# Output projection of a hybrid attention layer as seven block products in place of eight

## The chip, the cores and the metric

The kernel runs on one core of a Trainium2 chip. The metric is the device time of one execution in microseconds (us), lower is better. TensorE is written PE, VectorE DVE, ScalarE ACT, GpSimd POOL and SyncE SP, as in the profile.

## What is computed

One decoder layer on 512 tokens of width 1024, in fp32 (cut to what matters):

```python
def hybrid_layer(x, p_i, norm_g, w_in, sinks, rel_bias, w_out, ple_g, w_ple_gate, w_ple_proj):
    h = rms_norm(x, norm_g)
    proj = h @ w_in
    a_q, a_k, a_v, a_g, b_q, b_k, b_v, b_g = jnp.split(proj, offs, axis=-1)
    a_out = swa_attention(a_q, a_k, a_v, sinks, rel_bias[:, :8])      # window 128, 8 query heads
    b_out = moba_attention(b_q, b_k, b_v, rel_bias[:, 8:])            # blocks of 256, 8 heads
    mixed = jnp.concatenate([a_out * jax.nn.silu(a_g), b_out * jax.nn.silu(b_g)], axis=-1)
    x = x + mixed @ w_out                                             # (512 x 1024) @ (1024 x 1024)
    gate = jax.nn.sigmoid(rms_norm(x, ple_g) @ w_ple_gate)
    return x + (p_i @ w_ple_proj) * gate
# reference(): one such layer, then rms_norm(x, final_norm)
```

The change concerns `mixed @ w_out`, the output projection.

## The kernel before, in words

**Products of fp32.** Every fp32 operand is cut into two fp32r tiles: `hi`, a rounded copy, and `lo`, what is left. A product is then three matmuls (`three`, L136): hi by hi, hi by lo, lo by hi, added in one PSUM bank. One matmul takes a 128x128 stationary piece (128 tokens of 128 rows of K) and 512 columns.

**Weights** (class `Weights`, L85). `load` has SP fetch a raw block of 1 MB (128 x 2048 elements) into one of the two buffers of pool `wraw`. `split` cuts a quarter of it: ACT copies it into `hi` (L116) and DVE subtracts to get `lo` (L118). With `engines="AP"` every second `lo` cut goes to POOL instead; the default is `"AD"`.

**Stages.** (1) RMSNorm of x, its transposes, first columns of the input projection. (2) The rest of the input projection, 88 pieces of which stand in the list `stream`, woven into the attention: `run` takes the next pieces off the list, and `Pace` says how many after each step of attention, first 20 steps of the sliding-window attention (`swa_step`), then 38 of the block-sparse one (`moba_step`). A sliding-window step is a chain over all engines: scores on PE (L562), softmax with its normalisation on POOL (the "norm add" below, L574: the sum with the sink's term) and DVE (L575, L577), transposes on PE (L585), the product with V on PE (L602). Results go to the tiles `O`, and `silu_gate` (L539) multiplies them with the gate, six of the eight times on POOL. (3) The output projection: the gated `O` are split into `acts`; then eight K chunks of `w_out` times four token tiles times two halves of 512 columns times three matmuls, 192 in all. First the left half of the columns with four banks open and the K loop outside (`accs`), then the right half token tile by token tile. Each token tile then is added to x (`x2_evac`, L861), squared and normalised (`h2_norm`, L867), and transposed on PE (`h2_trans`, L874) while the next tile's matmuls run. Between the matmuls `ahead3` (L837) splits the next weights. (4) The gate projection on the same pattern, sigmoid, the last norm, the store.

**What sets the order.** PE's and SP's instructions stand in the order of the program (`MANUAL`, L34); DVE's, ACT's and POOL's are ordered by a scheduler when the kernel is built. Each engine works through its own queue in order, so a waiting instruction holds up all that stands behind it. A DMA waits at the engine that issues it: SP for all loads, POOL for the ten moves of `kt` (L514).

Of the kernel before, what the change touches and what calls it, by code (L numbers as in the profile page):

```python
# [10 lines left out]
F32 = mybir.dt.float32  # L11
# [5 lines left out]
P = 128  # L17
# [21 lines left out]
def hybrid_layer_kernel(  # L39
# [45 lines left out]
    class Weights:  # L85


        def __init__(self, name, srcs, a=KC, pool=None, cuts=4, engines="AD"):
            self.name, self.srcs, self.a, self.cuts, self.engines = name, srcs, a, cuts, engines
            self.pool = pool or whl  # L90
            self.done, self.raw, self.flat = 0, None, None

        def load(self):
            if self.raw is not None:
                return
            self.raw = wraw.tile([P, 2048], F32, name="raw_" + self.name, tag="raw")
# [39 lines left out]
    def three(acc, sh, sl, mh, ml, first, last):  # L136
        nc.tensor.matmul(acc, sh, mh, start=first, stop=False)  # L137
        nc.tensor.matmul(acc, sh, ml, start=False, stop=False)  # L138
        nc.tensor.matmul(acc, sl, mh, start=False, stop=last)  # L139
# [13 lines left out]
    d_tab = dram.tile([HA + HB, JT], F32, name="d_tab")  # L153

# [232 lines left out]
    opool = ctx.enter_context(ExitStack())  # L387
    with ExitStack() as ph2:
# [13 lines left out]
        O = [op.tile([P, SEQ], F32, name=f"O_{c}") for c in range(8)]  # L402
# [299 lines left out]
        make_va(akv[1])  # L702

# [103 lines left out]
        for c in range(KC):  # L807
            if c >= 6:
                silu_gate(c)
            split_T(acts[:, c, 0, :], acts[:, c, 1, :], O[c])  # L810


    with ExitStack() as ph3:
        def pool3(name, bufs):
            return ph3.enter_context(tc.tile_pool(name=name, bufs=bufs, reuse_waits="tile"))

        whl2 = pool3("whl2", 2)
        xq = pool3("xq", 1)
        ep = pool3("ep", 2)

        g_ple = xq.tile([P, D], F32, name="g_ple")
        nc.sync.dma_start(g_ple, bcast(ple_norm, D))
        g_fin = xq.tile([P, D], F32, name="g_fin")
        nc.sync.dma_start(g_fin, bcast(final_norm, D))
        x2 = []
        for t in range(NT):
            x_t = xq.tile([P, D], F32, name=f"x2_{t}")
            nc.sync.dma_start(x_t, x2d[t])
            x2.append(x_t)
        h2 = xq.tile([P, KC, 2, SEQ], F32R, name="h2")  # L830
# [175 lines left out]
```

## Time and profile before

| | |
|---|---|
| device time, median of 3 runs | 315.89 us (315.51 to 315.95) |
| the profiled execution | 315.71 us, of which the span of the profile is 314.0 us |
| PE busy, mean granted clock | 304.7 us (97% of the span), 0.996 |
| DVE, ACT, POOL busy | 219.3, 187.6 and 57.9 us |
| DMA | 37.61 MB, 120 GB/s over the span |
| output projection | first matmul at 215.85 us, first matmul of the gate projection at 262.05 us |

The span runs from the first to the last instruction that the profile shows. PE is busy almost all of it, and its busy time is pipelined: a matmul that is shown with 0.39 us starts 0.23 us after the one before it, so counts are to be multiplied with the distance of starts, not with durations.

### The profile page before, as it was taken

To read this page: it belongs to the slowest core of one execution; us is meant where nothing else is said; L and a number is where in the kernel's file an instruction comes from. 1 tells how busy PE (TensorE), PEld (TensorE's weight loads), DVE (VectorE), ACT (ScalarE), POOL (GpSimd) and SP (SyncE) were. 2 spreads that over 40 slices of the span, in tenths; PEclk is the share of its full clock that TensorE was granted. 3 is DMA by queue.
4 is the path that set the end of the run, shared out by engine and by line. 5 is a ranking of instruction groups with operands and counts; after the bars stand their busy time and mean duration, and the time that the engine had idled before them with its cause. 6 is when DMAs were issued, how large, how long until landed. Compare 5 with 4: busy or idle time off the path is not lost.

```text
span 314.0 us, 4729 instructions
## 1 busy us (share of the span) xinstructions
PE 304.7 (97%) x1651; PEld 260.5 (83%) x1651; DVE 219.3 (70%) x514; ACT 187.6 (60%) x420; POOL 57.9 (18%) x112
## 2 busy tenths in 40 slices
PE   8999999999999999999999999999999999999991
PEld 6788788888899878899888888888888888888890
DVE  2885867888877877478879797759167756582544
ACT  3756657656574865578668697798058323651441
POOL 1430102434544284100000100030000110000010
PEclk9999999999999999999999999999999999999998
DMA  6953487140405061951442603003965610000113
GB/s 217 400 188 106 144 223 228 46 136 1 134 3 200 3 177 23 265 163 45 134 100 50 187 0 137 0 0 91 397 234 221 208 58 0 2 0 0 69 68 134
DMA packets 33208, 37.61 MB, mean 120 GB/s; under 512 B 1416, under 2 KB 24976, under 8 KB 33184
## 3 DMA queue, kind: packets, MB, share of 16 engines
q1 hardware_dynamic: 32240, 34.47, 33.6%
q0 software_dynamic: 800, 2.62, 3.6%
q8 instruction: 13, 0.21, 0.3%
q10 hardware_dynamic: 144, 0.21, 0.2%
q14 instruction: 11, 0.09, 0.1%
HBM read 32.52 MB, written 2.16 MB: 110 GB/s over the span
## 4 chain that ended last, share of the span: by engine, by line
PE 82%; DVE 5%; ACT 4%; issue 4%; POOL 2%; DMA 1%; SPq 0%; ACTq 0%; POOLq 0%
PE acc L457 10%; PE acc L458 10%; PE acc L459 10%; PE acc L137 8%; PE acc L138 8%; PE acc L139 8%; PE acc_ple L284 4%; PE acc_akv L303 4%; PE oaccb L652 3%; PE Sb L622 3%; PE tpb L642 3%; PE S L562 2%; PE accv L137 2%; PE accv L139 2%; PE accv L138 2%
## 5 line engine op out<-in xcount | busy, mean ns | idle before, releaser
L137 PE MATMUL acc<-hi_wg,h 128*128 128x512 f32 (+1 forms) x72 | 26.5, 368 | 0.0
L138 PE MATMUL acc<-lo_wg,h 128*128 128x512 f32 (+1 forms) x72 | 26.3, 366 | 0.0
L139 PE MATMUL acc<-hi_wg,h 128*128 128x512 f32 (+1 forms) x72 | 26.3, 366 | 0.0
L457 PE MATMUL acc<-acts,hi_bkq 128*128 128x512 f32 x64 | 25.5, 399 | 0.0
L457 PE MATMUL acc<-acts,hi_aqg 128*128 128x512 f32 x64 | 25.4, 396 | 0.0
L458 PE MATMUL acc<-acts,hi_bkq 128*128 128x512 f32 x64 | 25.1, 393 | 0.0
L459 PE MATMUL acc<-acts,lo_bkq 128*128 128x512 f32 x64 | 25.1, 393 | 0.0
L137 PE MATMUL acc<-hi_wo,acts 128*128 128x512 f32 x64 | 25.1, 393 | 0.0
L458 PE MATMUL acc<-acts,hi_aqg 128*128 128x512 f32 x64 | 25.0, 391 | 0.0
L459 PE MATMUL acc<-acts,lo_aqg 128*128 128x512 f32 x64 | 24.9, 390 | 0.0
L139 PE MATMUL acc<-hi_wo,acts 128*128 128x512 f32 x64 | 24.9, 390 | 0.0
L138 PE MATMUL acc<-lo_wo,acts 128*128 128x512 f32 x64 | 24.9, 389 | 0.0
L625 ACT ACTIVATE stb<-stb,nmb 128x128 f32<-128x128 f32 (+3 forms) x32 | 17.9, 558 | 4.6 <-DVE nmb L623 4.2
L593 POOL TENSOR_SCALAR_AFFINE_SELECT pta<-pta 128x512 fp32r<-128x512 f32 x24 | 16.9, 705 | 17.6 <-DVE pta L144 15.8
L144 DVE TENSOR_TENSOR pt<-tpb,pt 128x384 fp32r<-128x384 f32 (+1 forms) x24 | 14.4, 600 | 7.6 <-ACT pt L143 7.4
L143 ACT ACTIVATE pt<-tpb 128x384 fp32r<-128x384 f32 (+1 forms) x24 | 12.6, 524 | 10.7 <-PE tpb L642 10.5
L137 PE MATMUL accv<-hi_bv,acts 128*128 128x256 f32 x64 | 18.4, 287 | 0.4 <-DVE q L505 0.4
L568 ACT ACTIVATE st<-st,nm 128x257 f32<-128x257 f32 (+1 forms) x32 | 15.2, 477 | 5.8 <-DVE nm L565 5.8
L139 PE MATMUL accv<-hi_bv,acts 128*128 128x256 f32 x64 | 18.1, 283 | 0.0
L138 PE MATMUL accv<-lo_bv,acts 128*128 128x256 f32 x64 | 18.1, 282 | 0.0
L850 ACT ACTIVATE sq<-x 128x512 f32<-128x512 f32 x15 | 9.5, 631 | 14.1 <-DVE x L912 11.2
L514 POOL DMA_DIRECT2D kt<-kt x10 | 5.5, 553 | 64.4 <-DVE kt L144 61.3
(166 smaller groups left out, 858.1 us busy)
## 6 DMA issues: line engine op xcount, KB each, us to landing
raw_aqg<-in_w_in_dram SPq DMA_DIRECT2D x8, 512.0 KB, 4.9
raw_bkq<-in_w_in_dram SPq DMA_DIRECT2D x8, 512.0 KB, 4.6
raw_wo<-in_w_out_dram SPq DMA_DIRECT2D x4, 1024.0 KB, 8.2
raw_wg<-in_w_ple_gate_dram SPq DMA_DIRECT2D x4, 1024.0 KB, 5.0
kt<-kt POOLq DMA_DIRECT2D x10, 256.0 KB, 3.2
x_t<-in_x_dram SPq DMA_DIRECT2D x4, 512.0 KB, 7.8
raw_bv<-in_w_in_dram SPq DMA_DIRECT2D x2, 1024.0 KB, 5.2
b_b<-d_tab SPq DMA_DIRECT2D x8, 256.0 KB, 5.6
```

Of the source, the lines that this page charges most:

```text
L137: nc.tensor.matmul(acc, sh, mh, start=first, stop=False)
L138: nc.tensor.matmul(acc, sh, ml, start=False, stop=False)
L139: nc.tensor.matmul(acc, sl, mh, start=False, stop=last)
L143: nc.scalar.activation(hi, src, AF.Copy)
L144: nc.vector.tensor_sub(lo, src, hi.bitcast(F32))
L284: nc.tensor.matmul(pacc[t, n], (pTl if j == 1 else pTh)[:, k, tok(t)], (wpl if j == 2 else wph)[:, n, k], start=k == 0 and j == 0, stop=k ...
L457: nc.tensor.matmul(acc, w.hi[:, k, cs], acts[:, k, 0, :], start=k == 0, stop=False)
L458: nc.tensor.matmul(acc, w.hi[:, k, cs], acts[:, k, 1, :], start=False, stop=False)
L459: nc.tensor.matmul(acc, w.lo[:, k, cs], acts[:, k, 0, :], start=False, stop=k == KC - 1)
L568: last_exp[0] = nc.scalar.activation(st[:, s, lo_k:257], st[:, s, lo_k:257], AF.Exp, bias=nm[:, s:s + 1], scale=-1.0, accum_out=sm[:, s:s ...
L593: nc.gpsimd.affine_select(out=pt[:, :, b, :].rearrange("p j (s q) -> p j s q", s=2), in_=pt[:, :, 1, :].rearrange("p j (s q) -> p j s q", ...
L625: last_exp[0] = nc.scalar.activation(st[:, :w], st[:, :w], AF.Exp, bias=nm, scale=-1.0, accum_out=sm)
```

## The change

The output projection is taken as a product of 2 x 2 blocks: tokens in two halves of 256, K and columns in two halves of 512 each. In place of eight block products it makes seven, of sums and differences of blocks (Strassen's scheme in the form that shares sums). With X the gated activations and W the blocks of `w_out`:

- Four weight sums are made in DRAM, in `d_sum` 1 to 4 (512x512 fp32, 1 MB each). SP copies a block there, DRAM to DRAM; POOL then adds another block by an accumulating DMA. `d_sum2` starts as a copy of `d_sum1`, `d_sum4` as one of `d_sum2`. These six steps (`sum_steps`) are put between the pieces of `stream`, at the places 16, 30, 60, 76, 160 and 172.
- Four differences of activation blocks are made on POOL (`sub`, L961): eight subtractions of 128x2x256 elements. `operand` then cuts each block that a product takes into hi and lo (ACT and DVE), some of it during the products. `O` becomes one tile `mixed`.
- Seven products `w1, w2, w5, w6, w3, w7, w4`, each two token tiles by four K chunks by three matmuls: 168 in place of 192, still of 512 columns. The accumulators of `w1` go on under `w6`, `w7` and `w4`, those of `w5` under `w3`; a partial result is added into x where each product ends, so 14 additions to x in place of 8.
- The raw loads are seven blocks of 1 MB in place of four, in one pool more (`wraw2`). For `w5, w6, w3, w7, w4` and the gate's weights every second `lo` cut goes to POOL (`engines="AP"`).

The core of the diff:

```diff
+    def sum_steps():
+        add = ALU.add
+        return [
+            lambda: (nc.sync.dma_start(d_sum[1], wo_block(0, 1)), nc.sync.dma_start(d_sum[3], wo_block(1, 1))),
+            lambda: (nc.gpsimd.dma_start(d_sum[1], wo_block(0, 0), accum_op=add),
+                     nc.gpsimd.dma_start(d_sum[3], wo_block(0, 1), accum_op=add)),
+            lambda: nc.sync.dma_start(d_sum[2], d_sum[1]),
+            lambda: nc.gpsimd.dma_start(d_sum[2], wo_block(1, 1), accum_op=add),
+            lambda: nc.sync.dma_start(d_sum[4], d_sum[2]),
+            lambda: nc.gpsimd.dma_start(d_sum[4], wo_block(1, 0), accum_op=add),
+        ]
...
+        steps = dict(zip((16, 30, 60, 76, 160, 172), sum_steps()))
...
+    def operand(dst, src, neg=False):
+        for h in range(2):
+            ks = slice(2 * h, 2 * h + 2)
+            hi, lo = dst[:, 0, ks, :], dst[:, 1, ks, :]
+            nc.scalar.activation(hi, src[:, ks], AF.Copy, scale=-1.0 if neg else 1.0)
+            if neg:
+                nc.vector.scalar_tensor_tensor(lo, src[:, ks], -1.0, hi.bitcast(F32), op0=ALU.mult, op1=ALU.subtract)
+            else:
+                nc.vector.tensor_sub(lo, src[:, ks], hi.bitcast(F32))
...
-        for c in range(KC):
-            if c >= 6:
-                silu_gate(c)
-            split_T(acts[:, c, 0, :], acts[:, c, 1, :], O[c])
+        operand(parts(slot[0]), X[0][0], True)
+        for c in (6, 7):
+            silu_gate(c)
+        operand(parts(slot[1]), X[0][1])
...
+        w5, w6 = summed(1, whl2, wraw2), summed(2, whl2, wraw2)
+        w3 = wide(wo, 1, "wo", engines="AP")[1]
+        w7, w4 = summed(3, whl, wraw), summed(4, whl2, wraw2)
...
+        def sub(dst, a, b):
+            for h in range(2):
+                ks = slice(2 * h, 2 * h + 2)
+                nc.gpsimd.tensor_sub(dst[:, ks], a[:, ks], b[:, ks])
+
+        def product(w, n, accs, fresh, evac, work):
+            a = parts(slot[n])
+            for i in range(2):
+                ts = tok(i)
+                for k in range(4):
+                    three(accs[i], a[:, 0, k, ts], a[:, 1, k, ts], w.hi[:, k], w.lo[:, k], fresh and k == 0, k == 3, go_on=not fresh)
+                    for f in work.get(4 * i + k, ()):
+                        f()
+                evac(i, accs[i])
...
-        accs = [bank([P, 512], "acc3", "S" if t < 2 else "acc") for t in range(NT)]
-        for k in range(KC):
-            for t in range(NT):
-                row_piece(accs[t], acts, w_late[0], t, k)
-            ahead3(1)
...
+        ab, gh = pair("S"), pair("acc")
+        product(w1, 0, ab, True, lambda i, acc: x2_add(i, 0, acc, neg=True),
+                {0: [lambda: sub(x11, x21, x11), a1], 1: [lambda: sub(x21, x21, x22)], 2: [a1], 4: [a1], 6: [a1]})
+        product(w2, 1, gh, True, lambda i, acc: x2_add(i, 0, acc, done=True),
+                {0: [lambda: operand(parts(slot[2]), x21)], 1: [a1], 2: [lambda: operand(parts(slot[0]), x22, True)],
+                 3: [lambda: sub(x22, x22, x11), a1], 5: [a1], 7: [a1]})
+        ef = pair("o")
+        product(w5, 2, ef, True, lambda i, acc: x2_add(2 + i, 1, acc),
+                {0: [lambda: operand(parts(slot[3]), x22)], 1: [lambda: sub(x12, x12, x22), a1], 3: [a1], 5: [a1],
+                 7: [a1]})
+        product(w6, 3, ab, False, lambda i, acc: x2_add(i, 1, acc),
+                {0: [lambda: operand(parts(slot[4]), x12)], 1: [a1], 3: [a1], 4: [lambda: operand(parts(slot[1]), x11)],
+                 5: [a1], 7: [a1]})
...
+        product(w3, 4, ef, False, evac3, {0: [a1], 2: [a1], 4: [a1], 6: [a1]})
+        product(w7, 1, ab, False, lambda i, acc: x2_add(2 + i, 1, acc, done=True),
+                {1: [a1], 3: [a1], 4: [tr], 5: [a1], 7: [a1]})
...
+        product(w4, 0, ab, False, evac4, {0: [tr], 1: [a1], 3: [a1], 5: [a1], 7: [a1]})
```

Three places of the queues, as the builds of the two kernels order them. The first is POOL's queue in the sliding-window attention. `st` is a step's softmax tile, `nsink` the sink's term, `pta` the transposed weights of the attention; L574 before is L613 after, L559 is L598. Before:

```order
L574 TENSOR_TENSOR st_611<-st_611 128x2x128
L559 COPY st_849<-nsink_81 128x2
L574 TENSOR_TENSOR st_650<-st_650 128x2x128
L559 COPY st_895<-nsink_81 128x2
L593 AFFINE_SELECT pta_711<-pta_711 128x2x256
```

After:

```order
L613 TENSOR_TENSOR st_613<-st_613 128x2x128
L185 DMA d_sum1_85<-in_w_out_dram 512x512
L186 DMA d_sum3_87<-in_w_out_dram 512x512
L598 COPY st_853<-nsink_81 128x2
L613 TENSOR_TENSOR st_652<-st_652 128x2x128
L598 COPY st_899<-nsink_81 128x2
L632 AFFINE_SELECT pta_713<-pta_713 128x2x256
```

Two accumulating DMAs have come between the norm adds of two successive steps; each waits at POOL until SP's copy into the same `d_sum` has landed. The third, into `d_sum2`, stands further on, right ahead of the norm add of `st_853`.

The second is SP's queue at the same time: the loads of raw weights and of bias tables (`b_a`). Before:

```order
L100 DMA raw_aqg3_598<-in_w_in_dram 128x8x128 x2
L100 DMA raw_bv0_737<-in_w_in_dram 128x8x256
L417 DMA b_a_739<-d_tab_84 128x2x256
L100 DMA raw_bkq0_934<-in_w_in_dram 128x8x128 x2
L100 DMA raw_bkq1_1096<-in_w_in_dram 128x8x128 x2
```

After:

```order
L100 DMA raw_aqg3_598<-in_w_in_dram 128x8x128 x2
L184 DMA d_sum1_85<-in_w_out_dram 512x512
L184 DMA d_sum3_87<-in_w_out_dram 512x512
L100 DMA raw_bv0_741<-in_w_in_dram 128x8x256
L456 DMA b_a_743<-d_tab_84 128x2x256
L100 DMA raw_bkq0_938<-in_w_in_dram 128x8x128 x2
L187 DMA d_sum2_86<-d_sum1_85 16x16384
L100 DMA raw_bkq1_1101<-in_w_in_dram 128x8x128 x2
```

The two first copies stand right behind the load of `raw_aqg3`; the copy of `d_sum1` to `d_sum2`, which waits for the accumulation into `d_sum1`, stands between the loads of `raw_bkq0` and `raw_bkq1`.

The third is POOL's queue from the last gates of the attention on. `rs` are sums of squares of the norm. Before:

```order
L540 TENSOR_TENSOR O_4_483<-O_4_483,G_4_2362 128x512
L540 TENSOR_TENSOR O_5_484<-O_5_484,G_5_2473 128x512
L128 TENSOR_TENSOR rs_2819<-epst_80,ssq2_2817 128x1
L128 TENSOR_TENSOR rs_2825<-epst_80,ssq2_2823 128x1
```

After:

```order
L579 TENSOR_TENSOR mixed_461<-mixed_461,G_4_2369 128x512
L579 TENSOR_TENSOR mixed_461<-mixed_461,G_5_2481 128x512
L964 TENSOR_TENSOR mixed_461<-mixed_461 128x2x256 x4
L118 TENSOR_TENSOR lo_wos1_2709<-raw_wos1_2678,hi_wos1_2708 128x512 x2
L118 TENSOR_TENSOR lo_wos2_2756<-raw_wos2_2681,hi_wos2_2755 128x512 x2
L964 TENSOR_TENSOR mixed_461<-mixed_461 128x2x256 x4
L128 TENSOR_TENSOR rs_2777<-epst_80,ssq2_2775 128x1
L128 TENSOR_TENSOR rs_2801<-epst_80,ssq2_2799 128x1
L118 TENSOR_TENSOR lo_wos4_2901<-raw_wos4_2739,hi_wos4_2900 128x512 x2
L118 TENSOR_TENSOR lo_wo11_2820<-raw_wo11_2817,hi_wo11_2819 128x512 x2
L118 TENSOR_TENSOR lo_wos3_2862<-raw_wos3_2693,hi_wos3_2861 128x512 x2
L118 TENSOR_TENSOR lo_wg00_2962<-raw_wg00_2795,hi_wg00_2961 128x512 x2
```

Where POOL had only tiny sums to do, 18 elementwise operations on 128x512 elements with two operands in SBUF now stand in its queue (the names `wos1, wos2, wos4, wo11, wos3` are those of `w5, w6, w4, w3, w7`), and two more for `wg01` behind them.

## Rows read from the trace of the kernel before

**Rows 1.** The page: busy time of each engine, and PE's granted clock.
```profile
PE 304.7 (97%) x1651; PEld 260.5 (83%) x1651; DVE 219.3 (70%) x514; ACT 187.6 (60%) x420; POOL 57.9 (18%) x112
...
PEclk9999999999999999999999999999999999999998
```
**Rows 2.** The page: the chain that ended last, by engine.
```profile
PE 82%; DVE 5%; ACT 4%; issue 4%; POOL 2%; DMA 1%; SPq 0%; ACTq 0%; POOLq 0%
```
**Rows 3.** Busy time by stretch: us, PE, PEld, DVE, ACT, POOL, clock, DMA, GB/s.
```profile
220.00:225.00 5.00, 5.00 (x23) 4.13 (x22) 1.07 (x2) 0.00 (x0) 0.00 (x0) 1.00 1.02 401
310.00:314.00 4.00, 0.00 (x0) 0.00 (x0) 0.14 (x1) 0.23 (x1) 0.00 (x0) 0.71 0.34 131
```
**Rows 4.** Timeline of PE, output projection: start, us, instruction.
```profile
215.85 0.45 PE L137 MATMUL acc<-hi_wo,acts 128*128 128x512 f32 x1
...
224.10 0.39 PE L137 MATMUL acc<-hi_wo,acts 128*128 128x512 f32 x1
...
229.54 0.39 PE L137 MATMUL acc<-hi_wo,acts 128*128 128x512 f32 x1
...
262.05 0.48 PE L137 MATMUL acc<-hi_wg,h 128*128 128x512 f32 x1
```
**Rows 5.** The chain in order of time: start, us, what (three of its transposes).
```profile
59.24 0.24 PE tp L585 x2
...
76.64 0.24 PE tp L585 x2
...
248.75 0.87 PE tp L879 x8
```
**Rows 6.** Two-operand work of 128x512: POOL's by line (ns min/median/max), DVE's by timeline.
```profile
L540 POOL TENSOR_TENSOR O<-O,G x6: 1275/1294/1792, 111.2 to 208.5; 128x512 f32<-128x512 f32 x6
...
230.25 5.06 DVE L118 TENSOR_TENSOR lo_wo<-raw_wo,hi_wo 128x512 fp32r<-128x512 f32 x8 [9.19 <-ACT hi_wo L116]
```
**Rows 7.** Timelines of DVE and POOL where both work at once, 111 to 126 us.
```profile
111.17 1.41 DVE L577 TENSOR_SCALAR st<-st,ri 128x128 f32<-128x128 f32 x1 [1.16 <-POOL st L574]
111.19 1.30 POOL L540 TENSOR_TENSOR O<-O,G 128x512 f32<-128x512 f32 x1
115.08 0.69 DVE L144 TENSOR_TENSOR kt<-acc,kt 64x512 fp32r<-64x512 f32 x1 [0.33 <-ACT kt L143]
115.31 0.65 POOL L593 TENSOR_SCALAR_AFFINE_SELECT pta<-pta 128x512 fp32r<-128x512 f32 x1
123.91 0.69 DVE L118 TENSOR_TENSOR lo_bv<-raw_bv,hi_bv 128x512 fp32r<-128x512 f32 x1
123.97 1.79 POOL L540 TENSOR_TENSOR O<-O,G 128x512 f32<-128x512 f32 x1 [4.28 <-DVE O L612]
```
**Rows 8.** Timeline of SP's DMA queue in the sliding-window attention.
```profile
44.85 1.17 SPq L100 DMA_DIRECT2D raw_aqg<-in_w_in_dram  x2
...
64.32 16.28 SPq L100 DMA_DIRECT2D raw_bkq<-in_w_in_dram  x4
```
**Rows 9.** DMA issues: what, queue, count, KB each, median us to landing.
```profile
raw_aqg<-in_w_in_dram SPq DMA_DIRECT2D x8, 512.0 KB, 4.9
...
raw_wo<-in_w_out_dram SPq DMA_DIRECT2D x4, 1024.0 KB, 8.2
```
**Rows 10.** Timelines of POOL and DVE in the sliding-window attention.
```profile
50.37 0.93 POOL L574 TENSOR_TENSOR st<-st 128x256 f32<-128x256 f32 x1 [12.48 <-ACT st L568]
54.03 0.74 POOL L574 TENSOR_TENSOR st<-st 128x256 f32<-128x256 f32 x1 [1.74 <-ACT st L568]
54.81 0.48 DVE L577 TENSOR_SCALAR st<-st,ri 128x128 f32<-128x128 f32 x2 [0.43 <-POOL st L574]
...
70.60 0.73 POOL L574 TENSOR_TENSOR st<-st 128x256 f32<-128x256 f32 x1 [2.59 <-ACT st L568]
71.37 0.48 DVE L577 TENSOR_SCALAR st<-st,ri 128x128 f32<-128x128 f32 x2
```
**Rows 11.** The page's groups: POOL's own DMA issues.
```profile
L514 POOL DMA_DIRECT2D kt<-kt x10 | 5.5, 553 | 64.4 <-DVE kt L144 61.3
```

More of the change, by code (lines that the diff above doesn't have):

```diff
@@ L134, in rstd, with three @@
         return s
[L136 to L139, printed above, removed]
+    def three(acc, sh, sl, mh, ml, first, last, go_on=False):
+        nc.tensor.matmul(acc, sh, mh, start=first, stop=False, skip_group_check=go_on)
+        nc.tensor.matmul(acc, sh, ml, start=False, stop=False, skip_group_check=go_on)
+        nc.tensor.matmul(acc, sl, mh, start=False, stop=last, skip_group_check=go_on)
     def split_T(hi, lo, src):
@@ L702, in hybrid_layer_kernel @@
         make_va(akv[1])
+        items, n = deque(stream), 0
+        stream.clear()
+        steps = dict(zip((16, 30, 60, 76, 160, 172), sum_steps()))
+        for it in items:
+            if it[0]:
+                if n in steps:
+                    add(0, steps[n])
+                n += 1
+            stream.append(it)
         class Pace:
@@ L841, in ahead3 @@
                     w.split()
-                    nx = flat_late.index(w) + 1
-                    if w.done == w.cuts and nx + 1 < len(flat_late):
-                        flat_late[nx + 1].load()
+                    if w.done == w.cuts and id(w) in follows:
+                        follows[id(w)].load()
+        load_x(0)
+        w5.load()
+        load_x(1)
+        w6.load()
+        while split_seq[0] in (w1, w2):
+            ahead3(1)
+        load_x(2)
+        load_x(3)
+        nc.sync.dma_start(g_ple, bcast(ple_norm, D))
+        nc.sync.dma_start(g_fin, bcast(final_norm, D))
+        ssq = {}
         def square(t, key, cols):
-            sq = ep.tile([P, 512], F32, name="sq2", tag="sq", bufs=1)
+            sq = ep.tile([P, 512], F32, name="sq2", tag="sg")
             ss = small.tile([P, 1], F32, name="ssq2", bufs=12)
@@ L854, in half, with row_piece, x2_add @@
             return slice(n * 512, (n + 1) * 512)
[L856 removed]
+        def row_piece(acc, t, w, k, cols=slice(0, 512)):
             ww = w[k // 4]
[L858 removed]
+            three(acc, h2[t][:, k, 0, :], h2[t][:, k, 1, :], ww.hi[:, k % 4, cols], ww.lo[:, k % 4, cols],
                   k == 0, k == KC - 1)
[L861 to L863 removed]
+        def x2_add(t, n, acc, neg=False, done=False):
+            xs = x2[t][:, half(n)]
+            if neg:
+                nc.vector.tensor_sub(xs, xs, acc)
+            else:
+                nc.vector.tensor_add(xs, acc, xs)
+            if done:
+                square(t, 0, half(n))
+        h2 = [slot[(2, 3, 4, 1)[t]].rearrange("p (k j n) -> p k j n", k=KC, j=2) for t in range(NT)]
         h2t = {}
@@ new lines, in product, with pair @@
+        def product(w, n, accs, fresh, evac, work):
[7 more added lines that the diff above has]
+                evac(i, accs[i])
+        def pair(tag):
+            return [bank([P, 512], "acc3", tag) for _ in range(2)]
```

98 lines of the change are left out of this document (53 added, 45 removed).

## Prediction

> **What bounds the kernel now.** The page comes first: PE is busy for 97% of the span, at full granted clock in every slice but the last [rows 1], and the chain that ended last runs 82% through PE [rows 2]. So a matmul that is left out ends the kernel earlier by one distance of starts, as long as the other engines have PE's operands ready. That distance is read from PE's timeline in the stage that changes [rows 4]: from 224.10 to 229.54 us lie 24 matmuls, 5.44 us, 0.2267 each. The whole stage, 215.85 to 262.05, is 46.2 us; 192 x 0.2267 is 43.5, and three blocks of transposes of 0.87 [rows 5] make 46.1. PE waits for nothing there; whatever becomes late there is paid in full.
>
> The second view is what the other engines do beside it. POOL is busy for 18% of the span [rows 1], so it looks free. What a POOL operation costs and what it does to DVE stands in rows 6 and 7. POOL's six multiplications of 128x512 with two operands in SBUF took 1.275 us at the least, DVE's subtractions of that size 5.06 / 8 = 0.63 [rows 6]. Where they meet they take turns [rows 7]: a DVE operation of 128x128, of which two take 0.48 elsewhere [rows 10], started 0.02 ahead of such a POOL operation and took 1.41, until that had ended; a POOL operation that started 0.06 behind a DVE subtraction took 1.79. A DVE subtraction with one operand in PSUM beside POOL kept its 0.69. So POOL's time on such work is not beside DVE's two-operand time, it is added to it.
>
> The third view is the sliding-window attention, where new DMAs are put. POOL's norm add of a step ends at 54.77, DVE's scaling at 55.29 [rows 10], and PE takes the transposes at 59.24 [rows 5]: 3.95 us of slack. For a later step, 71.85 to 76.64, it is 4.8 us.
>
> **The sum, part by part**, against the profiled execution, 315.71 us (span 314.0 and 1.71 around it), 0.18 under the median of 315.89.
>
> 1. *Matmuls.* 24 fewer at 0.2267: **-5.44**. The new stage asks PE for 168 x 0.2267 = 38.1 and two blocks of transposes, 39.8 us; the third block moves to the gate's stage and is no gain.
>
> 2. *POOL and DVE in the stage.* POOL gets 8 subtractions, 12 `lo` cuts and 2 for `wg01`: 22 x 1.275 = 28.1 us. DVE keeps two-operand work of 35 pieces: 4 cuts of w2, 14 of the seven later blocks, 12 in `operand`, one gate, four of the norms; at 0.63 that is 22.1. In turns this is 50.1 us against PE's 39.8: **+10.2**. Nothing is added for DVE's evacuations from PSUM (six more than before at 0.69 [rows 7], hidden beside POOL's time), nor for ACT's 12 more copies, ACT being busy for 60% [rows 1]. Ends: 0 if the two work side by side after all (28.1 and 22.1 both fit into 39.8), and +21.6 if each POOL operation takes the longest, 1.79 [rows 6]: 39.4 + 22.1 - 39.8 is 21.7. I take the middle value, since the rows show turns; the two meetings of rows 7 lost 0.1 to 0.2 less than full turns, 3 us over 22, but a queue of 57 pieces with PE's order behind it doesn't pack without gaps either, so I credit nothing.
>
> The Trainium skill (SBUF — State Buffer, "Who interferes with whom") says of the port pair that DVE and GpSimd share that it is an exclusive lock: a DVE instruction with two inputs in SBUF and a GpSimd instruction that reads SBUF exclude each other for a whole instruction, while DVE with one SBUF input outside its two-port modes is untouched. The trace agrees, with the 1.41 and 1.79 against the unlengthened 0.69 [rows 7]. By that rule POOL's 18% is no sign of room; read without it, the term would be 0 and the sum 10.2 lower.
>
> 3. *Waits in the stage.* `w4` and `w7` go on in the bank that was just added into x, and x's last halves come with the last two products, so norm and transposes of two token tiles crowd the end. SP asks for the raw block of `w3` only behind two loads that wait for buffers; loads land 5 to 8 us after the issue [rows 9], and `w3` is the fifth product, 21.8 us (4 x 5.44) into the stage. **+1**, ends 0 and +3 (one evacuation, 0.69, behind a POOL operation, 1.28 [rows 6, 7], at one or two such places).
>
> 4. *First stall.* SP's two first copies stand right behind `raw_aqg3`, issued at 44.85 and at 46.02 out of SP's queue [rows 8]; with 4.9 us to landing [rows 9] that load is in at about 50.3 us (second half). No row shows a DRAM to DRAM copy. Its nearest rows are loads: 401 GB/s was the rate with the engines full [rows 3], 1 MB in 2.6 us. A copy that reads and writes by the same engines takes twice that, 5.2, so the second one lands near 60.7. POOL issued the norm add of `st_613` at 50.37 [rows 10] and then meets two DMAs that wait for those copies; two issues at 0.55 [rows 11] later, at 61.5, comes the norm add that had ended at 54.77, and ends at 62.2: 7.5 late. If only its own chain were late PE would lose 7.5 - 3.95 = 3.5; but DVE stands behind the same norm add in order, with the evacuations of the projection in its queue, so up to 7.5 is lost. **+5**. Ends: a copy in 2.6 puts the second landing at 55.5, the norm add 2.6 late, cost 0; a copy at the pace of `raw_wo`, 8.2 [rows 9], puts it at 66.7, 13.6 late: +13.
>
> The Trainium skill (DMA: Bandwidth & Descriptors, "Latency and other measured facts") gives 207 to 214 GB/s for copies between HBM tensors; the estimate by it is 5.0 us for 1 MB, and the sum would be some 0.4 lower by it. No run here shows such a copy.
>
> 5. *Second stall.* An accumulation reads two blocks and writes one, three times 2.6 or 7.9 us, so that of `d_sum1` is done about 60.7 + 7.9 = 68.6. SP waits for it with the copy to `d_sum2` behind `raw_bkq0` (64.32 [rows 8]) and holds up `raw_bkq1`; the copy lands at 73.8, or 76.4 with 2.6 for `raw_bkq0` ahead of it. POOL waits with the accumulation, and behind it the norm add of 70.60 [rows 10]. Issue, norm add and scaling from 76.4 on end at 78.2; PE, 5 late already, wants the transposes at 81.6. So the likely cost is small, **+2**, ends 0 and +12 (copies and accumulations at 8.2 per MB: 66.7 + 12.3 + 8.2 = 87.2, against 76.64 + 7 or so). The later pair of steps (`d_sum4`) stands where POOL has almost nothing to do; 0, covered by the third quarter of the attention.
>
> Sum: -5.44 + 10.2 + 1 + 5 + 2 = +12.8, or **328.5 us**. Three MB more of raw blocks and 7 MB or more of DRAM traffic cost nothing by themselves: the engines moved 120 GB/s on the mean against 401. A lower clock after a stall is not in the sum; the one stretch without matmuls shows 0.71 [rows 3], and four microseconds at that after each stall would cost 1.2 each, inside the range.
>
> **Rivals.**
> A. *The port decides, the copies are hidden* (terms 4 and 5 zero): 315.71 - 5.44 + 11.2 = 321.5. For it: 3.95 us of slack, and the DMA engines are half idle there. Against: POOL's queue in order.
> B. *The stalls decide, the port work is hidden*: -5.44 + 1 + 7 gives 318.3. For it: the POOL work could start early, while the last attention steps still run; against: rows 7.
> C. *Faster*: both are covered, and the seven products earn what they save, 315.71 - 5.44 + 1 + a little = 312. This is decided by two bounds together: each copy under about 3.2 us (so that the second lands before 56.8, when the norm add is no more than 3.95 late), and POOL's 28.1 and DVE's 22.1 overlapping by more than 10. For it: DVE's operations that meet POOL's can be the ones that read PSUM. Against: more than half of what DVE does in the stage has two operands in SBUF.
> D. *Both stalls at their high ends*: +10 to +20 more, 338 to 350.
>
> **How the numbers follow.** Forecast, 324 to 335: 0.45. A 0.15, B 0.12, D 0.12, C 0.12, and 0.04 for a result within 0.2% (0.6 us), about what a measurement of this kernel can tell from no change. Faster is C, 0.12; slower is the rest, 0.84. The range takes in A, B and the forecast and half of D: 317 to 344, which leaves out C and the upper half of D, 0.18.
>
> **What the profile of the changed kernel would show.** Right: 168 matmuls in the stage with gaps between them, the releaser DVE or POOL `lo` and L964; POOL's two-operand work at 1.3 or more and DVE's `lo` cuts lengthened beyond 0.63; POOL idle 8 or more us ahead of L185 or L186 with a DMA as the releaser, and PE waiting at L585's successor around 60 us. Wrong: a stage of about 40 us without gaps (then term 2 is nothing), or the norm add of the second step within 4 us of its old time (then term 4 is nothing), or PE gaps in a place that no term names, such as `w3`'s weights.

## The result, and the profile after

The changed kernel takes 333.44 us (median of 4 runs, 332.88 to 333.76); the kernel before took 315.92 beside it. The ratio is 1.0555 (95% interval 1.0537 to 1.0573): 17.5 us slower. The profiled execution has a span of 331.7 us against 314.0, so 17.7 us are to be found.

The page, with the answer to [rows 1]:

```profile
PE 307.1 (93%) x1627; PEld 259.5 (78%) x1627; DVE 240.5 (72%) x520; ACT 197.4 (60%) x438; POOL 103.6 (31%) x142
...
PEclk9999999899999999999999999999996989999998
```

PE has 24 instructions fewer and POOL 46 us more. What [rows 1] did not show is in the second row: three dips of the granted clock inside the kernel.

First and last rows of the output projection on PE's timeline, as in [rows 4]:

```profile
225.01 0.45 PE L138 MATMUL acc<-hi_wo,acts 128*128 128x512 f32 x1
...
278.87 0.39 PE L138 MATMUL acc<-hi_wg,acts 128*128 128x512 f32 x1
```

With the 215.85 and 262.05 of [rows 4] the 17.7 us fall into three parts:

| | before | after | difference |
|---|---|---|---|
| up to the first matmul of the projection | 215.85 | 225.01 | +9.16 |
| the projection | 46.20 | 53.86 | +7.66 |
| the gate projection and the rest | 51.95 | 52.83 | +0.88 (one block of transposes, 0.87, moved there) |

What PE waited for, the longest first (us in total, times, longest):

```profile
PE S L601 <- DVE q L544: 3.9, 1, 3.9
PE acc L139 <- DVE lo_wo L118: 3.7, 1, 3.7
PE acc L138 <- DVE x L937: 2.6, 1, 2.6
PE accv L138 <- DVE Vb L145: 2.4, 1, 2.4
PE tp L624 <- DVE st L616: 1.2, 2, 0.7
```

Every long wait ends at DVE. The first, the fourth and the fifth lie in the attention, the second and the third in the projection.

**The first stall.** Timeline of POOL from 50 us on (start, us, instruction, idle time before it and its releaser), the answer to [rows 10]:

```profile
49.98 0.93 POOL L613 TENSOR_TENSOR st<-st 128x256 f32<-128x256 f32 x1 [12.48 <-ACT st L607]
55.94 1.12 POOL L185 DMA_DIRECT2D d_sum<-in_w_out_dram  x1 [5.03 <-DMA d_sum<-in_w_out_dram]
59.37 1.01 POOL L186 DMA_DIRECT2D d_sum<-in_w_out_dram  x1 [2.30 <-DMA d_sum<-in_w_out_dram]
60.01 0.56 POOL L598 COPY st<-nsink 128x2 f32<-128x2 f32 x1
60.15 1.09 POOL L613 TENSOR_TENSOR st<-st 128x256 f32<-128x256 f32 x1
```

POOL stands still until SP's copies have landed, at 55.9 and 59.4, and the norm add that had ended at 54.77 ends at 61.24. DVE, in the same time:

```profile
53.83 0.17 DVE L614 RECIPROCAL ri<-sm 128x2 f32<-128x2 f32 x1
61.27 0.48 DVE L616 TENSOR_SCALAR st<-st,ri 128x128 f32<-128x128 f32 x2 [7.28 <-POOL st L613]
61.79 0.69 DVE L544 SCALAR_TENSOR_TENSOR q<-acc,q 64x512 fp32r<-64x512 f32 x1
```

and PE:

```profile
58.29 0.33 PE L601 MATMUL S<-kt,q 128*128 128x128 f32 x2
62.53 0.44 PE L601 MATMUL S<-kt,q 128*128 128x128 f32 x2 [3.91 <-DVE q L544]
62.81 0.40 PE L624 MATMUL tp<-rev,st 128*128 128x128 f32 x2
...
63.44 0.63 PE L496 MATMUL acc<-acts,hi_aqg 128*128 128x512 f32 x1
63.87 0.63 PE L497 MATMUL acc<-acts,hi_aqg 128*128 128x512 f32 x1
```

PE did not wait for the late transposes but for the evacuation of `q`, which stood behind the late scaling in DVE's queue. After the gap matmuls start 0.43 us apart, not 0.2267: the lower of the two clock levels, 1.2 GHz. Rows by stretch, of the gap and of what follows it (us, PE, PEld, DVE, ACT, POOL, clock, DMA, GB/s):

```profile
58.60:62.50 3.90, 0.03 (x1) 0.00 (x0) 1.17 (x3) 0.00 (x0) 2.00 (x4) 1.00 1.06 189
62.50:66.50 4.00, 3.96 (x14) 3.29 (x15) 2.68 (x9) 2.89 (x8) 2.09 (x4) 0.57 1.14 209
```

The clock falls when PE is at work again: a mean of 0.57 over 4 us is 3.4 us at half, 1.7 us more. The stall cost 5.6 us.

**The second stall.** SP's queue, and POOL's:

```profile
70.79 1.52 SPq L100 DMA_DIRECT2D raw_bkq<-in_w_in_dram  x2
72.35 0.97 SPq L187 DMA_DIRECT2D d_sum<-d_sum  x1
```
```profile
73.86 0.19 POOL L598 COPY st<-nsink 128x2 f32<-128x2 f32 x1
80.27 1.03 POOL L188 DMA_DIRECT2D d_sum<-in_w_out_dram  x1 [6.23 <-DMA d_sum<-d_sum]
80.96 1.10 POOL L613 TENSOR_TENSOR st<-st 128x256 f32<-128x256 f32 x1
```

The norm add of 70.60 [rows 10] now starts at 80.96, 10.4 late, while PE takes the transposes of 76.64 [rows 5] at 82.53, 5.9 late. The difference of 4.5 us used up nearly all of the 4.8 us of slack. PE waits 0.54 us at once, and at 104.75, 22 us later, 2.43 us for an evacuation of `Vb` that DVE reaches at 104.28. Neither wait is in the profile of the run without weight sums, so both come with the sums; that DVE had no slack left in between is the likely link and was not followed step by step.

```profile
82.53 0.50 PE L624 MATMUL tp<-rev,st 128*128 128x128 f32 x2 [0.54 <-DVE st L616]
...
104.75 0.39 PE L138 MATMUL accv<-hi_bv,acts 128*128 128x256 f32 x1 [2.43 <-DVE Vb L145]
```

**The projection.** Busy time by stretch, first of the kernel before, then of the changed one:

```profile
215.85:262.05 46.20, 46.20 (x219) 38.49 (x218) 28.41 (x44) 20.20 (x44) 3.12 (x10) 1.00 0.59 205
```
```profile
225.01:278.87 53.86, 45.49 (x187) 35.30 (x186) 49.22 (x54) 31.23 (x64) 37.87 (x31) 0.90 0.42 145
```

DVE is busy for 49 of 54 us and POOL for 38, and the mean clock is 0.90. What the busy time is made of shows in the lines of the `lo` cuts and of the differences (ns min/median/max):

```profile
L118 POOL TENSOR_TENSOR lo_wos<-raw_wos,hi_wos x8: 1712/1734/1782, 230.1 to 256.3; 128x512 fp32r<-128x512 f32 x8
L118 DVE TENSOR_TENSOR lo_wos<-raw_wos,hi_wos x8: 679/1177/1782, 232.3 to 257.4; 128x512 fp32r<-128x512 f32 x8
...
L964 POOL TENSOR_TENSOR mixed<-mixed x8: 1287/1704/1746, 220.4 to 243.8; 128x512 f32<-128x512 f32 x8
```

A POOL piece takes 1.7 us where [rows 6] had 1.28, a DVE cut up to 1.78 where it had 0.63. (POOL's queue after the change, as listed above, holds 20 such pieces, not 18, and with the two for `wg01` 22. The first three differences ran at 220.4 to 225.1, ahead of the projection.) Both timelines side by side, DVE and then POOL:

```profile
249.00 2.85 DVE L118 TENSOR_TENSOR lo_wos<-raw_wos,hi_wos 128x512 fp32r<-128x512 f32 x2
251.78 0.68 DVE L937 TENSOR_TENSOR x<-acc,x 128x512 f32<-128x512 f32 x1
252.38 2.84 DVE L118 TENSOR_TENSOR lo_wo<-raw_wo,hi_wo 128x512 fp32r<-128x512 f32 x2
255.14 1.77 DVE L118 TENSOR_TENSOR lo_wos<-raw_wos,hi_wos 128x512 fp32r<-128x512 f32 x1
```
```profile
247.84 3.46 POOL L118 TENSOR_TENSOR lo_wos<-raw_wos,hi_wos 128x512 fp32r<-128x512 f32 x2 [1.11 <-ACT hi_wos L116]
251.27 3.40 POOL L118 TENSOR_TENSOR lo_wo<-raw_wo,hi_wo 128x512 fp32r<-128x512 f32 x2
```

In each 3.4 us there are two POOL cuts, two DVE cuts and one addition into x with an operand in PSUM, which keeps its 0.68. The Trainium skill (SBUF — State Buffer, "Who interferes with whom") has the rule for this, an exclusive lock for whole instructions that spares a DVE instruction with only one input in SBUF, outside its two-port modes; these rows agree with it on both counts.

PE waits three times for about a microsecond or more in this stage, at 248.4 and 249.9 (1.0 and 3.7 us, for the cuts of `w3`, whose block SP asked for at 241.46, 16.4 us into the projection) and at 267.9 (2.6 us, for an addition into x that must empty the bank for `w4`). After the second and the third the clock is down again:

```profile
253.59:257.59 4.00, 4.00 (x9) 3.13 (x10) 4.00 (x4) 1.45 (x3) 4.00 (x3) 0.50 0.14 48
271.00:275.00 4.00, 3.85 (x16) 2.93 (x15) 3.87 (x6) 3.52 (x9) 2.07 (x3) 0.57 0.00 0
```

4 us at 0.50 and 4 at 0.57 are 2.0 and 1.7 us of PE's time.

### The profile page after: what moved, and what is told of

The parts are those of the page before. It is cut to its first block, busy times and chain, and to the rows that moved or that the text cites. A ratio compares the mean times of both kernels' runs of the same rounds, so it can differ in the third digit from the quotient of the medians.

```text
span 331.7 us, 4774 instructions
## 1 busy us (share of the span) xinstructions
PE 307.1 (93%) x1627; PEld 259.5 (78%) x1627; DVE 240.5 (72%) x520; ACT 197.4 (60%) x438; POOL 103.6 (31%) x142
## 5 line engine op out<-in xcount | busy, mean ns | idle before, releaser
L496 PE MATMUL acc<-acts,hi_aqg 128*128 128x512 f32 x64 | 26.0, 407 | 0.0
L497 PE MATMUL acc<-acts,hi_aqg 128*128 128x512 f32 x64 | 25.5, 399 | 0.0
L616 DVE TENSOR_SCALAR st<-st,ri 128x128 f32<-128x128 f32 x32 | 11.9, 414 | 15.9 <-POOL st L613 15.8
L138 PE MATMUL acc<-hi_wg,acts 128*128 128x512 f32 (+1 forms) x56 | 20.2, 360 | 0.0
L140 PE MATMUL acc<-hi_wg,acts 128*128 128x512 f32 (+1 forms) x56 | 20.1, 359 | 0.0
L139 PE MATMUL acc<-lo_wg,acts 128*128 128x512 f32 (+1 forms) x56 | 20.1, 359 | 0.0
L579 POOL TENSOR_TENSOR mixed<-mixed,G 128x512 f32<-128x512 f32 x6 | 8.2, 1371 | 29.8 <-ACT G L584 25.5
L662 DVE CUSTOM_DVE_ANT_0 stb<-Sb,b_b 128x128 f32<-128x128 f32 (+3 forms) x32 | 15.6, 486 | 2.0 <-PE Sb L661 1.5
```

The costliest lines, as they stand in the source:

```text
L138: nc.tensor.matmul(acc, sh, mh, start=first, stop=False, skip_group_check=go_on)
L139: nc.tensor.matmul(acc, sh, ml, start=False, stop=False, skip_group_check=go_on)
L140: nc.tensor.matmul(acc, sl, mh, start=False, stop=last, skip_group_check=go_on)
L496: nc.tensor.matmul(acc, w.hi[:, k, cs], acts[:, k, 0, :], start=k == 0, stop=False)
L497: nc.tensor.matmul(acc, w.hi[:, k, cs], acts[:, k, 1, :], start=False, stop=False)
L662: nc.vector.tensor_tensor_reduce(st[:, :w], S[:, :w], bias[:, 512 - w:], -1.0, 1.0e38, ALU.add, ALU.min, nm)
```

## The experiments

Times are medians. The kernel before took 315.9 us beside the changed kernel and 315.6 to 315.7 beside the other runs. The ratios are to it; they are taken over all runs and can differ a little from the quotient of two medians. "Projection" runs from its first matmul to the first of the gate projection in the profiled execution.

| run | time, us | ratio (95% interval) | projection starts | lasts |
|---|---|---|---|---|
| changed kernel | 333.44 | 1.0555 (1.0537 to 1.0573) | 225.01 | 53.86 |
| no weight sums | 324.28 | 1.0267 (1.0247 to 1.0287) | 216.16 | 53.94 |
| copies, no accumulation | 323.24 | 1.0247 (1.0225 to 1.0269) | 215.60 | 52.81 |
| sums later | 324.39 | 1.0276 (1.0259 to 1.0294) | 215.40 | 54.42 |
| w3 asked for early | 333.85 | 1.0579 (1.0560 to 1.0598) | 224.90 | 54.06 |
| POOL's work left out | 322.36 | 1.0203 (1.0176 to 1.0230) | 227.12 | 41.14 |
| sums later, all on DVE | 316.33 | 1.0009 (0.9993 to 1.0025) | 215.50 | 46.62 |
| sums later, cuts on DVE | 315.61 | 1.0013 (0.9994 to 1.0032) | 215.74 | 44.97 |
| the same, w3 early | 317.58 | 1.0052 (1.0032 to 1.0073) | 215.92 | 45.58 |
| the same, wide cuts | 315.57 | 0.9997 (0.9981 to 1.0013) | 215.89 | 45.31 |
| wide cuts, w3 not early | 320.04 | 1.0139 (1.0121 to 1.0156) | 217.30 | 49.79 |
| wide cuts, first operands narrow | 315.00 | 0.9982 (0.9973 to 0.9991) | 215.51 | 44.93 |
| before, half of its later cuts on POOL | 316.38 | 1.0031 (1.0015 to 1.0046) | 215.64 | 47.14 |

### Is it the sums that cost the nine microseconds ahead of the projection?

```diff
-        steps = dict(zip((16, 30, 60, 76, 160, 172), sum_steps()))
+        steps = {}
...
-            return Weights(f"wos{i}", [d_sum[i].rearrange("(k p) c -> p k c", p=P)], a=4, pool=pool, rpool=rpool,
+            blk = {1: wo_block(0, 1), 2: wo_block(1, 1), 3: wo_block(0, 1), 4: wo_block(1, 0)}[i]
+            return Weights(f"wos{i}", [blk.rearrange("(k p) c -> p k c", p=P)], a=4, pool=pool, rpool=rpool,
```

> Leaves out the weight sums: no DMA from DRAM to DRAM, no accumulating DMA, and w5, w6, w7, w4 load plain blocks of w_out of the same size. Theory (POOL and, behind it, DVE wait in order for the copies): the output projection starts at about 216.0 us in place of 225.0, its length stays near 54 us, the time falls by 9 to about 324.5 (323 to 326). Rival (the loss ahead of the projection comes from something else, such as the moved loads or the slots between the pieces of the stream): the start stays past 222 us and the time at 330 or more.

Measured 324.28, with the projection from 216.16 on and 53.94 us long. The sums cost 9.2 us. In the profiles 8.9 of these are the earlier start, and the projection keeps its length to 0.1.

### POOL's wait, or the traffic of the copies?

```diff
-            lambda: (nc.gpsimd.dma_start(d_sum[1], wo_block(0, 0), accum_op=add),
-                     nc.gpsimd.dma_start(d_sum[3], wo_block(0, 1), accum_op=add)),
+            lambda: None,
...
-            lambda: nc.gpsimd.dma_start(d_sum[2], wo_block(1, 1), accum_op=add),
+            lambda: None,
...
-            lambda: nc.gpsimd.dma_start(d_sum[4], wo_block(1, 0), accum_op=add),
+            lambda: None,
```

> The changed kernel with SP's four copies where they are and no accumulating DMA; leaves out the second summand of each weight sum. Theory (POOL's queue behind the waits is the stall, not the copies' traffic nor SP's queue): the output projection starts at 215.5 to 217 us, time 323.5 to 326. Rival (the copies, lying between the loads of the attention's weights, delay these): start at 219 or later, time 328 or more.

Measured 323.24, just under the expected range, projection from 215.60 on. SP's copies in the same place cost nothing that can be seen. This run takes the accumulations' own traffic away too, and SP's third copy has no accumulation to wait for any more; the next run puts all of it back.

```diff
-        steps = dict(zip((16, 30, 60, 76, 160, 172), sum_steps()))
+        steps = dict(zip((114, 126, 150, 160, 168, 175), sum_steps()))
```

> The same sums, with the six steps at the pieces 114, 126, 150, 160, 168 and 175, where POOL has little to do. Theory (what costs is POOL's queue behind the copies, not the traffic): projection starts at 216 to 218 us, time 324.5 to 327, within 2 us of the run without sums. Rival (the 7 MB and more of DRAM traffic cost time wherever they lie, by slowing the loads): start past 221 us, time 329 or more.

Measured 324.39, projection from 215.40 on, both a little below what was expected: same copies, same accumulations, 9 us less. With the run before it this shows that it was the place in POOL's queue that cost the time, between two norm adds of a step chain, and not the traffic.

### The place of w3's load, or the port?

The longest gap in the projection lies ahead of the product `w3`, whose raw block SP asks for late. This run asks for it early:

```diff
-        follows = {id(w): v for w, v in ((w1, w3), (w2, w7), (w5, w4), (w6, wga[0]), (w3, wga[1]), (w7, wgb[0]),
+        follows = {id(w): v for w, v in ((w5, w4), (w6, wga[0]), (w3, wga[1]), (w7, wgb[0]),
...
         w6.load()
+        w3.load()
...
         nc.sync.dma_start(g_fin, bcast(final_norm, D))
+        w7.load()
```

> The raw block of w3 is asked for right behind those of w5 and w6, and that of w7 after the loads of x and of the gains; all else as in the changed kernel. Theory A (the place of the load on SP makes w3 late): the gaps of 1.0 and 3.7 us ahead of the product w3 go, with them the stretch at the lower clock; time 326 to 329. Theory B (the backlog of POOL and DVE on their shared port makes w3 late, whatever the load does): the gap moves or shrinks by less than 2 us; time 331 to 333.5.

Measured 333.85, just above the range of theory B. Neither theory holds whole: the gap ahead of `w3` is gone, as A had it, and yet no time is gained, as B had it. The waits come up elsewhere, as its timeline of PE shows.

```profile
244.32 0.50 PE L140 MATMUL acc<-hi_wos,acts 128*128 128x512 f32 x1 [2.18 <-DVE acts L426]
...
258.11 0.47 PE L138 MATMUL acc<-hi_wos,acts 128*128 128x512 f32 x1 [2.15 <-DVE x L939]
...
264.58 1.12 PE L958 MATMUL tp<-ident,h_t 128*128 128x128 f32 x4 [2.79 <-DVE h_t L950]
```

All of them are waits for DVE again, the projection is 54.06 us long, and DVE is busy for 49.5 of it. The waits moved and their sum stayed, which speaks for DVE as the engine that is full.

The next run leaves POOL's two-operand work out and gives ACT stand-ins of the same size (those for the cuts don't wait for `hi`, so the chain to the operands is shorter too):

```diff
-            e = nc.gpsimd if self.engines[1] == "P" and self.done % 2 else nc.vector
-            e.tensor_sub(lo[:, sl], self.raw[:, sl], hi[:, sl].bitcast(F32))
+            if self.engines[1] == "P" and self.done % 2:
+                nc.scalar.activation(lo[:, sl], self.raw[:, sl], AF.Copy, scale=0.0)
+            else:
+                nc.vector.tensor_sub(lo[:, sl], self.raw[:, sl], hi[:, sl].bitcast(F32))
...
-                nc.gpsimd.tensor_sub(dst[:, ks], a[:, ks], b[:, ks])
+                nc.scalar.activation(dst[:, ks], a[:, ks], AF.Copy)
```

> Leaves out what POOL does with two operands in SBUF during the output projection: the eight differences of activation blocks become copies on ACT, and the lo cuts that POOL had become zeros written by ACT. Theory (POOL and DVE take turns): DVE's lo cuts fall to 0.6 to 0.7 us each, the projection from 53.9 to 41 to 46 us (the late load of w3 may keep a few us of gap), time 321 to 326. Rival (the order of the loads and of the accumulators sets the projection, and the port is only slack): projection 50 us or more, time 330 or more.

Measured 322.36. Its busy time over the projection:

```profile
227.12:268.26 41.14, 40.69 (x187) 32.99 (x186) 33.11 (x53) 40.21 (x83) 3.18 (x9) 1.00 0.53 189
```

41.14 us, at full clock, with PE busy for 40.69 of them, and no gap ahead of `w3`. Its load stands where the changed kernel has it, but SP came to it 13.3 us into the projection in place of 16.4. DVE does its 53 instructions in 33.1 us where the 54 of the changed kernel took 49.2; its `lo` cuts of these weights take 0.67 to 0.70 us each. So 12.7 us of the projection (53.86 - 41.14) came with POOL's two-operand work, the gap at `w3` among them. (The first stall is longer in this profile, 5.3 us in place of 3.9, which makes most of the later start.)

### Can the work be placed so that the seven products pay?

The sums stay late; first DVE takes all of POOL's pieces, then only the cuts, with the eight differences left on POOL.

```diff
-                           engines="AP")
+                           engines="AD")
...
-                nc.gpsimd.tensor_sub(dst[:, ks], a[:, ks], b[:, ks])
+                nc.vector.tensor_sub(dst[:, ks], a[:, ks], b[:, ks])
```

The first line is meant for all blocks that had it; the second change is in the first of the two runs alone.

> The late sums, and in the output projection DVE does all that POOL had there: the eight differences and every lo cut. Theory (work in turns on a shared port, POOL's pieces twice as dear): DVE was busy for 33.1 us of the projection without POOL's 22 pieces; 22 more at 0.63 make 47, so the projection is bound by DVE at 47 to 50 us in place of 54.4, time 317 to 321. Rival (what counts is that DVE has too much to do, wherever POOL's share lies): projection 53 us or more, time 323 or more.

> The late sums; the lo cuts go back to DVE, the eight differences stay on POOL. Theory: on the port 49 pieces of 0.63 and 8 of 1.28 make 41 us, DVE alone 33.1 + 14 x 0.63 = 42, against 39.8 of PE: projection 43 to 47 us, time 313 to 317, within 2 us of the kernel before. Rival (eight POOL pieces at the start of the chain of operands are as harmful as 22): projection 50 us or more, time 320 or more.

Measured 316.33 and 315.61, projections of 46.62 and 44.97 us: 8 to 9 us below the run with late sums, and neither to be told from the kernel before. The first is a little faster than expected. DVE alone does in 46.6 us what DVE and POOL did in 54.4, so POOL's help cost 7.8 us more than it gave; the 5.5 us from 41.1 to 46.6 are what the same work costs on DVE. The row of the second:

```profile
215.74:260.71 44.97, 41.14 (x186) 32.94 (x186) 43.79 (x66) 30.90 (x63) 12.59 (x14) 1.00 0.48 174
```

DVE is busy for 43.8 of 45.0 us, so it is likely the bound now. And `w3` is still late. SP came to its load 16.4 and 16.7 us into the projection, as late as in the changed kernel, and PE waited in the first run for its `hi` and in the second for its `hi` (0.8 us) and its `lo`:

```profile
240.87 0.79 PE L138 MATMUL acc<-hi_wo,more 128*128 128x512 f32 x1 [2.85 <-ACT hi_wo L116]
```
```profile
242.68 0.50 PE L139 MATMUL acc<-lo_wo,more 128*128 128x512 f32 x1 [2.02 <-DVE lo_wo L118]
```

So the gap ahead of `w3` does not need POOL's cuts: it came in runs where DVE was busy almost throughout, whether held up by POOL or by its own pieces, and it went where DVE was busy for only 33 of 41 us or the load was asked for early. Two variants tried to do better. Asking for `w3` early (the edit shown above, on the kernel with the cuts on DVE):

> As the run before it, with the raw block of w3 asked for right behind those of w5 and w6. Theory (w3 was late by the port's backlog, which held up the buffer that the load ahead of it waits for): within 1 us of the run before it. Rival (with the backlog gone the load's place is what makes w3 late): 1 to 3 us faster than it.

Measured 317.58, 2 us slower by the medians (1.2 by the ratios); neither expectation held. The waits of 0.8 and 2.0 us ahead of `w3` went, and waits of 1.2 us at the transposes and 1.9 us for an addition into x came, with DVE busy for 43.9 of 45.6 us. This profile is of the fastest run, 316.04, so what the slower ones lost is not in it. Why the runs lie between 316.0 and 318.1 was not settled.

Cuts of 1024 columns in place of 512, half as many, with `ahead3` called half as often:

```diff
-        for h in range(2):
-            ks = slice(2 * h, 2 * h + 2)
+        for h in range(1):
+            ks = slice(0, 4)
...
-                           engines="AD")
+                           cuts=2, engines="AD")
```

> Late sums, lo cuts on DVE, w3 asked for early, and DVE's and ACT's cuts of the late blocks and of the operands twice as wide (128x1024). Two cuts of 128x512 take 1.28 us on DVE, 0.64 each, of which about 0.1 is not spent on elements if 512 elements take 0.53; 20 cuts fewer free 2 us of DVE. Theory (DVE, busy without a gap from 216 to 247 us, bounds the projection now): 2 to 3 us faster than the same with narrow cuts, 313.5 to 315.5. Rival (wider cuts are ready later for the first matmul that needs them, and the wait eats the gain): 316 or more.

> The same with w3 asked for where the changed kernel has it. Theory (DVE bounds): 313 to 315, 1 to 3 us faster than with narrow cuts (315.6). Rival (the load's place): a gap of 2 us or more ahead of w3 stays, 315 or more.

With `w3` early 315.57, just above what was expected, 2 us below the same with narrow cuts; without, 320.04, with a gap of 4 us ahead of `w3`, as the rival had it. Here the load's place does cost time, 4.5 us. It cost none in the changed kernel, and with narrow cuts on DVE the early load was the slower one; why the three pairs differ was not settled. In the first of the two PE waited 1.84 us for the second operand, so its cut was made narrow again (`operand(..., n=2)` for the first two operands):

> As the run with wide cuts and w3 asked for early, but the first two operands (ready at the end of the attention) are cut in narrow halves again. Theory (there PE waited 1.84 us for the second half of the second operand, and ran some us at the lower clock after it): that gap goes, the rest stays; 312.8 to 314.5, faster than both kernels. Rival (DVE is as busy as before, and the wait turns up at the next product): 315 to 316.

Measured 315.00, ratio 0.9982 (0.9973 to 0.9991): just faster than the kernel before, by 0.6 us, which is at the edge of what can be told. The time is in the rival's range, and so is the reason: the gap at the second operand went, and waits of 1.3 and 1.5 us came in `w6` instead.

```profile
215.51:260.44 44.93, 42.15 (x187) 34.23 (x186) 42.77 (x47) 29.92 (x45) 12.96 (x14) 0.96 0.52 172
```

The projection is no shorter than with narrow cuts and DVE is still busy for 42.8 of 44.9 us. But the clock is 0.96 here, where it was 1.00 with narrow cuts: by that mean 1.8 us of the 44.9 are the lower clock after the waits in `w6`. Without it the projection would take about 43.1, an estimate; the wide cuts may have won what the clock took back. This is the best version found.

### Does POOL's help hurt where there is room?

```diff
-        w_late = [late, wide(wo, 1, "wo", whl2), wide(wg, 0, "wg"), wide(wg, 1, "wg", whl2)]
+        w_late = [late, wide(wo, 1, "wo", whl2, engines="AP"), wide(wg, 0, "wg", engines="AP"),
+                  wide(wg, 1, "wg", whl2, engines="AP")]
```

> The kernel before, with every second lo cut of the second half of w_out's columns and of the gate's weights on POOL. Theory (the sum on the port against PE's time decides): in the output projection DVE was busy for 28.4 us; 8 cuts fewer at 0.63 and 8 on POOL at 1.28 to 1.75 make 34 to 38 of 46 us, so PE still waits for nothing: 315.2 to 316.8. Rival (a POOL cut is late for PE by its own length, 1.7 in place of 0.63): 317 or more.

Measured 316.38, ratio 1.0031 (1.0015 to 1.0046), as expected but for one wait of PE: 0.47 us for a norm behind POOL's cuts. The projection is 47.14 us long in place of 46.20. Its row (up to 0.3 us ahead of the gate's first matmul):

```profile
215.64:262.50 46.86, 46.38 (x215) 38.12 (x215) 27.13 (x35) 20.38 (x43) 17.09 (x19) 1.00 0.56 202
```

POOL's nine pieces take 14 us more here, DVE with nine fewer is busy for only 1.3 us less, and it costs 0.7 us: DVE, busy for 27 of 47 us, has room for being held up, which it had not where POOL's 22 pieces cost 12.7 us.

## Why the prediction was right, and where its sizes were off

The forecast was 328.5, the range 317 to 344, slower with 0.84; measured 333.44. The likeliest case came, port and stalls together, by the two mechanisms that were written down.

1. *Matmuls, -5.44.* Right. With POOL's work out of the way the projection takes 41.14 us where the forecast's bare PE time was 39.8.

2. and 3. *Port and waits in the stage, +11.2.* Measured 14.1 (53.86 - 39.8); 3.7 of this is the lower clock after two gaps, and 10.4 without it. That this is so near has luck in it. The 50.1 us of the port took POOL's pieces at 1.28 and DVE's at 0.63, and the sum has a slip of 0.1 (50.1 - 39.8 is 10.3). Measured, POOL's pieces took 1.7 us each. What PE waited for was DVE with all its work, 49.2 busy us, and not the two-operand part of both engines; without POOL's pieces 33.1 of the 49.2 remain. Also, the 1.41 us of [rows 7] is a DVE operation with one tensor operand, so by that reading not only DVE's two-operand work is held up. The lateness of `w3` was booked as a matter of its load (ends 0 and +3). The runs show both: the gap goes when the load is asked for early, and when DVE is relieved, and in the changed kernel only the second gains time.

4. *First stall, +5.* Measured 3.9 of waiting and 1.7 of lower clock. The copies landed at 55.9 and 59.4 us where the working had 55.5 and 60.7, from loads alone, and the norm add was 6.5 late, not 7.5 (the working also counted two issues behind the second landing, where one stands). That DVE's queue, with the projection's evacuations in it, would be what PE waits for came as this term had it, and not as the list of signs had it, which named the transposes.

5. *Second stall, +2.* Measured about 3.3: 0.54, 2.43, and 0.3 more at 123 us. The forecast compared one norm add with one slack and found it covered. The slack was spent by it, and the wait turned up 22 us later at an instruction that the working did not look at.

Without the clock the waits of terms 2 to 5 come to 17.6 us against 18.2 in the sum, with misses of -0.8, -1.1 and +1.3 that nearly cancel. What the sum lacked is in the sentence after it, that a lower clock after a stall is not in it. The clock took 1.7 + 2.0 + 1.7 = 5.4 us, and the time came out 4.9 above the forecast. The three stretches at half clock lasted about 3.4, 4 and 3.4 us of PE's work, each worth half its length, 1.7 to 2.0 in place of the 1.2 that was named and left out.

Of the signs, POOL's idle time ahead of the two accumulations was 7.3 us (5.03 and 2.30), not 8 or more. And one of the signs of being wrong came: PE's longest gap in the projection, 3.7 us, is ahead of `w3`'s weights. The stated range also leaves out a result within 0.2% of no change (0.04), so what lay inside it had 0.78, and 0.22 and not 0.18 lay outside.

Rival A's time, 321.5, is near the runs without sums or with late ones (324.3), its excess again being the stage's 14 for 11. Rival B's, 318.3, answers to the run without POOL's work (322.4), where the stalls alone cost more than 7 (start at 227.1). Rival C did not come, and the experiments say what it would have taken: sums out of the step chain's way and no two-operand work on POOL. Subtracting the two effects, 333.4 - 9.0 - 12.7, gives 311.7, near its 312; but that run would have no one to make the cuts. With DVE making them 315.0 was the least.

The estimate by the Trainium skill (DMA: Bandwidth & Descriptors, "Latency and other measured facts"), 5.0 us for a copy of 1 MB, can be put beside rows now. The figure on that page is for tiles of 128 rows of 16 KiB at a favourable row pitch, which the prediction did not say; the two copies here have 512 rows of 2 KB. The second copy landed 3.4 us after the first, the two being in flight together behind a load. In the run with late sums the last copy, issued at 177.01 with nothing issued by SP for 6.9 us before it, landed after 7.3 us, its start-up included. The traces don't contradict the rate and don't settle it.

## What to carry to other kernels

Before work goes to an idle engine, ask what it shares and who has time left. Here an engine at 18% could take over 8 pieces with no loss that can be told, and not 22, since its pieces ran in turn with those of the engine it was to help, at 1.7 us for what that one does in 0.65. A DMA that waits is an instruction in someone's queue: place it by what stands behind it. Its landing time can be estimated from rows of loads: here that came within 1.3 us. When removing a wait gains nothing and other waits on the same engine appear, suspect that the engine is full, and count its busy time. A sum of waits wants a term for the clock after each of them.

## What was not expected of the hardware

- The granted clock fell to its lower level after gaps of 3.9, 3.7 and 2.6 us of PE, each time when PE was at work again; the gap of 2.4 us that ends at 104.75 left it at 1.00 (first row below). The length of the gap alone does not decide it. With wide cuts the same gap of 1.84 us stands at the second operand in both runs; in the 5 us from its end on the clock was 0.66 in the run with `w3` early (second row) and 1.00 in the other (third row). What decides it is open.

```profile
100.00:130.00 30.00, 26.89 (x173) 23.98 (x172) 22.99 (x63) 21.04 (x51) 16.29 (x21) 1.00 0.36 106
```
```profile
223.87 0.50 PE L140 MATMUL acc<-hi_wo,acts 128*128 128x512 f32 x1 [1.84 <-DVE acts L426]
```
```profile
225.28 0.50 PE L140 MATMUL acc<-hi_wo,acts 128*128 128x512 f32 x1 [1.84 <-DVE acts L426]
```

- A meeting of POOL and DVE takes less than the sum: two POOL cuts and two DVE cuts in 3.4 us, 1.7 a pair, where 1.28 + 0.63 is 1.91.

- Accumulating DMAs are shown with 1.0 to 1.2 us at their issue on POOL, twice the 0.55 of [rows 11]. They don't hold POOL that long: the next instruction starts 0.64 us behind the one at 59.37 and 0.69 behind the one at 80.27. They land late (median us from issue, with the copies beside them):

```profile
d_sum<-in_w_out_dram POOLq DMA_DIRECT2D x4, 1024.0 KB, 10.5
...
d_sum<-in_w_out_dram SPq DMA_DIRECT2D x2, 1024.0 KB, 11.1
...
d_sum<-d_sum SPq DMA_DIRECT2D x2, 8.4
```

Open is what the smaller waits in the projection are made of. Gaps over 0.3 us (8.2) and the clock (3.7) make 11.9 of the 14.1 us; the rest was not followed.
